# High and low halves of the stationary operands, interleaved word by word in one tile

## The chip, the cores and the metric

The kernel runs on one core of a Trainium2 chip. The metric is the device time of one execution in microseconds (us); smaller is better. Names of engines: PE is TensorE (matmuls), PEld its weight loads, DVE is VectorE, ACT is ScalarE, POOL is GpSimd, SP is SyncE, which issues most DMAs.

## The reference

One pre-norm layer on an input of 256 tokens by 2048 channels, float32. Four token mixers read one combined projection, their outputs are projected, gated, summed, projected again and added to the input.

```python
h = _rms_norm(x, norm_g)
u = jnp.einsum('bsd,dn->bsn', h, w_in)              # 2048 -> 22672 columns
a_in, b_in, b_gate, c_qkv, c_f, c_gate, d_in, d_gate, m_logit = _split(u, IN_SIZES)
y_a = _short_conv_branch(a_in, conv_w)              # 1024 columns each
y_b = _rwkv7_branch(b_in, b_gate, ...)
y_c = _fox_branch(c_qkv, c_f, c_gate, fox_bf)
y_d = _pool_branch(d_in, d_gate, pool_w, pool_scale)
ys = jnp.stack([y_a, y_b, y_c, y_d], axis=2)
proj = jnp.einsum('bskc,kcd->bskd', ys, w_branch)   # four of 1024 -> 2048
gates = jax.nn.sigmoid(m_logit.reshape(bsz, s, N_BRANCH, d) + b_merge)
merged = jnp.sum(gates * proj, axis=2)
x = x + jnp.einsum('bsd,de->bse', merged, w_out)    # 2048 -> 2048
# and a final _rms_norm(x, final_g)
```

## The kernel before

The 256 tokens are two blocks of 128 (`NB = 2`). Activations are the stationary operand of every large matmul: a slice of 128 channels (k) by 128 tokens is loaded as weights. The weight matrices are the moving operand, 512 columns at a time (`CH`). Each such output of 256 tokens by 512 columns is a chunk (L247 `chunk`).

Float32 accuracy is had from a fast format, fp32r, by splitting each operand in a high part (the value rounded to fp32r) and a low part (the rest). A product of two split operands is made of three matmuls, high times high (L240), high times low (L241) and low times high (L242), which add up in one PSUM tile, `psm`. So a chunk of `w_in` has 16 slices k, two blocks and three products, 96 matmuls, each with a weight load of its own.

Where the high and low parts lie: the moving slices arrive by DMA in `raw` (L259, from SP's queue, two slices a DMA, three buffers), ScalarE rounds them to `wh` (L267) and VectorE subtracts to get `wl` (L268), six buffers each. The stationary parts are two tiles for each operand: `xh` and `xl` for the normalised input (written at L218 by ScalarE and L219 by VectorE, from the PSUM tiles of PE's transposes), and for the branch outputs `yah`, `yal` to `ydh`, `ydl` (L776), written by `split_T` (L771 ScalarE, L772 VectorE). The merged rows are split into `mh` and `ml` (L815, L816), which take the places of `yb`, `yc`, `ya` and a tile of their own, and L831 joins their parts. In all of these tiles the words of one slice lie one behind the other, so that a weight load of 128 words reads 512 bytes in one piece.

Order: the head loads and transposes `x` while the first chunk runs; then come the chunks of the branches, with the work of RWKV (L440) and of the attention (L641) between the chunks on all engines; then `split_T` of three branches and the pool branch (about 750 to 820 us); then the merge, 4 column groups (`dc`) of 4 branches, each with a gate chunk (L740) and a branch chunk of 8 slices (L821), and a `split_T` of 4 slices after each group (L828); last the output projection, 4 chunks (L855). The last of these keeps its split slices in tiles that have become free (`keep`, L847: `xh`, `xl`, `ych`, `ycl`, `ydh`, `ydl`), and runs its second block after its first. The residual `x` is loaded again into `yal` and `ybl` by GpSimd's queue (L842). A scheduler orders the instructions of each engine by priority; the preparation of the moving slices has the highest (`WEIGHTS`).

Of the kernel before, what the change touches and what calls it, by code (L numbers as in the profile page):

```python
# [9 lines left out]
F32 = mybir.dt.float32  # L10
F32R = mybir.dt.float32r
I32 = mybir.dt.int32
AF = mybir.ActivationFunctionType
ALU = mybir.AluOpType
# [3 lines left out]
P = 128  # L18
T = 256
NB = 2  # L20
D = 2048
W = 1024
CH = 512
# [71 lines left out]
def kernel(  # L95
# [27 lines left out]
    nc = tc.nc  # L123
    v = nc.vector
    sc = nc.scalar
# [5 lines left out]
    w_out_v = w_out[0].rearrange("(k p) n -> p k n", p=P)  # L131
# [3 lines left out]
    pers = ctx.enter_context(tc.tile_pool(name="pers", bufs=1))  # L135
    wpool = ctx.enter_context(tc.tile_pool(name="wpool", bufs=1))
    bc_pool = ctx.enter_context(tc.tile_pool(name="bc", bufs=2))
    ynat = ctx.enter_context(tc.tile_pool(name="ynat", bufs=1))
# [22 lines left out]
    ngT = pers.tile([P, D // P], F32, name="ngT")  # L161
# [2 lines left out]
    fss = pers.tile([P, NB, 4], F32, name="fss")  # L164
    frs = pers.tile([P, NB], F32, name="frs")
    fa = pers.tile([P, NB, 16], F32, name="fa")
    xh = pers.tile([P, D // P, T], F32R, name="xh")
    xl = pers.tile([P, D // P, T], F32R, name="xl")
    cst = pers.tile([P, N_CONST], F32, name="cst")

    def load_constants(lo, hi):
# [17 lines left out]
    def flat(t):  # L189
        return t.rearrange("p a b -> p (a b)")  # L190


    gp.memset(ones1, 1.0)

    rw_stack = ExitStack()
# [5 lines left out]
    def x_quarter(q):  # L201

        xt = xin.tile([P, NB, CH], F32, name=f"x{q}")
        nc.sync.dma_start(out=xt, in_=x_v[:, :, q * CH:(q + 1) * CH])
        if q == 0:
            tp = psum_ex("c")
            nc.tensor.transpose(tp[:, 0:16], ng16, ident[:16, :16])
            v.tensor_copy(out=ngT, in_=tp[:, 0:16])
        for k2 in range(2):
            tp = psum_ex("c" if k2 else "r")  # L210
            for j in range(2):
                for b in range(NB):
                    c0 = (2 * k2 + j) * P
                    nc.tensor.transpose(tp[:, j * T + b * P:j * T + (b + 1) * P], xt[:, b, c0:c0 + P], ident)
            for j in range(2):
                k = q * 4 + k2 * 2 + j
                s = tp[:, j * T:(j + 1) * T]
                sc.activation(out=xh[:, k, :], in_=s, func=AF.Copy, scale=ngT[:, k:k + 1])  # L218
                v.scalar_tensor_tensor(out=xl[:, k, :], in0=s, scalar=ngT[:, k:k + 1],  # L219
                                       in1=xh[:, k, :].bitcast(F32), op0=ALU.mult, op1=ALU.subtract)  # L220
        return xt

    def x_squares(q, xt):
# [12 lines left out]
    def products(ps, sth, stl, wh, wl, k, nk, n, b):  # L236
        cols = slice(b * P, (b + 1) * P)
        o = ps[b][:, :n]
        h, l = wh[:, :n], wl[:, :n]
        nc.tensor.matmul(o, lhsT=sth[:, k, cols], rhs=h, start=k == 0, stop=False)  # L240
        nc.tensor.matmul(o, lhsT=sth[:, k, cols], rhs=l, start=False, stop=False)  # L241
        nc.tensor.matmul(o, lhsT=stl[:, k, cols], rhs=h, start=False, stop=k == nk - 1)  # L242

    def new_ps():
        return [ps_main.tile([P, CH], F32, name="psm", tag="psm") for b in range(NB)]
# [1 line left out]
    def chunk(ranges, nk, sth, stl, before=lambda g: None, keep=None):  # L247


        ps = new_ps()  # L250
        n = sum(r[2] for r in ranges)
        for g in range(nk // KG):
            wh, wl = [], []
            with level(WEIGHTS):
                before(g)
                raw = wpool.tile([P, KG, CH], F32, name="raw", bufs=3)
                at = 0
                for wv, c0, w in ranges:
                    nc.sync.dma_start(out=raw[:, :, at:at + w], in_=wv[:, g * KG:(g + 1) * KG, c0:c0 + w])  # L259
                    at += w  # L260
                for j in range(KG):
                    if keep:
                        h, l = keep(g * KG + j)
                    else:
                        h = wpool.tile([P, CH], F32R, name="wh", bufs=6)
                        l = wpool.tile([P, CH], F32R, name="wl", bufs=6)
                    sc.activation(out=h[:, :n], in_=raw[:, j, :n], func=AF.Copy)  # L267
                    v.tensor_tensor(out=l[:, :n], in0=raw[:, j, :n], in1=h[:, :n].bitcast(F32), op=ALU.subtract)  # L268
                    wh.append(h)
                    wl.append(l)  # L270
            for b in range(1 if keep else NB):
                for j in range(KG):
                    products(ps, sth, stl, wh[j], wl[j], g * KG + j, nk, n, b)
        if keep:
            for k in range(nk):
                products(ps, sth, stl, *keep(k), k, nk, n, 1)
        return ps
# [47 lines left out]
    x_norm()  # L325
    rw_stack.close()

    yb = ynat.tile([P, NB, W], F32, name="yb")
    yc = ynat.tile([P, NB, W], F32, name="yc")
    ya = ynat.tile([P, NB, W], F32, name="ya")  # L330


    rw = rw_stack.enter_context(tc.tile_pool(name="rw", bufs=1))
# [5 lines left out]
    lo, hi = slice(0, 64), slice(64, 128)  # L339
# [419 lines left out]
    ytp = ctx.enter_context(tc.tile_pool(name="ytp", bufs=1))  # L759
    yT = {}  # L760

    def split_T(dst, k0, src, nk):

        for k2 in range(0, nk, 2):
            tp = psum_ex("r" if (k2 // 2) % 2 else "z")
            for j in range(2):
                for b in range(NB):
                    nc.tensor.transpose(tp[:, j * T + b * P:j * T + (b + 1) * P],
                                        src[:, b, (k2 + j) * P:(k2 + j + 1) * P], ident)
            hi = flat(dst[0][:, k0 + k2:k0 + k2 + 2, :])  # L770
            sc.activation(out=hi, in_=tp, func=AF.Copy)  # L771
            v.tensor_tensor(out=flat(dst[1][:, k0 + k2:k0 + k2 + 2, :]), in0=tp, in1=hi.bitcast(F32),  # L772
                            op=ALU.subtract)

    def new_yT(nm):
        yT[nm] = [ytp.tile([P, W // P, T], F32R, name=f"y{nm}{i}") for i in "hl"]  # L776
        return yT[nm]

    split_T(new_yT("a"), 0, ya, 8)
    split_T(new_yT("b"), 0, yb, 8)  # L780
# [4 lines left out]
    for hf in range(2):  # L785
# [4 lines left out]
        for g2 in range(2):  # L790
# [6 lines left out]
            for j in range(2):  # L797
                cs = slice((g2 * 2 + j) * P, (g2 * 2 + j + 1) * P)
                tp = psum_ex("c")
# [3 lines left out]
            tp = psum_ex("c")  # L803
            for b in range(NB):
                for j in range(2):
                    nc.tensor.matmul(tp[:, b * T:(b + 1) * T], lhsT=pT[:, j, b * P:(b + 1) * P], rhs=pw[:, j, :],
                                     start=(j == 0), stop=(j == 1))
# [4 lines left out]
        split_T(yTd, hf * 4, yd, 4)  # L812


    mh = [ynat.tile([P, 8, T], F32R, name=n) for n in ("yb", "yc")]  # L815
    ml = [ynat.tile([P, 8, T], F32R, name="ya"), ytp.tile([P, 8, T], F32R, name="ml1")]  # L816
    for dc in range(4):
        mg = wk.tile([P, NB, CH], F32, name="va")
        for n, nm in enumerate("abcd"):
            gt = gate_tile(dc, n)  # L820
            ps = chunk([(w_br_v[n], dc * CH, CH)], W // P, *yT[nm])  # L821
            for b in range(NB):
                if n == 0:
                    v.tensor_tensor(out=mg[:, b, :], in0=ps[b], in1=gt[:, b, :], op=ALU.mult)
                else:
                    v.tensor_tensor(out=gt[:, b, :], in0=ps[b], in1=gt[:, b, :], op=ALU.mult)
                    v.tensor_tensor(out=mg[:, b, :], in0=mg[:, b, :], in1=gt[:, b, :], op=ALU.add)
        split_T([mh[dc // 2], ml[dc // 2]], (dc % 2) * 4, mg, 4)  # L828


    class Parts:  # L831
        def __init__(self, parts):
            self.parts = parts

        def __getitem__(self, key):
            _, k, cols = key
            return self.parts[k // 8][:, k % 8, cols]

    yo = [ytp.tile([P, NB, 1024], F32, name=n) for n in ("yah", "ybh")]
    xr = [ytp.tile([P, NB, 1024], F32, name=n) for n in ("yal", "ybl")]  # L840
    for j in range(2):
        gp.dma_start(out=xr[j], in_=x_v[:, :, j * 1024:(j + 1) * 1024])  # L842

    spare = [t.rearrange("p a b -> p (a b)").rearrange("p (k n) -> p k n", n=CH)
             for t in (xh, xl, *(ytp.tile([P, W // P, T], F32R, name=n) for n in ("ych", "ycl", "ydh", "ydl")))]

    def keep(k):  # L847
        if k < 8:
            return spare[0][:, k, :], spare[1][:, k, :]
        i = 2 + 2 * ((k - 8) // 4)  # L850
        return spare[i][:, k % 4, :], spare[i + 1][:, k % 4, :]

    for dc in range(4):
        fg = bcast(final_g[dc * CH:(dc + 1) * CH])
        ps = chunk([(w_out_v, dc * CH, CH)], D // P, Parts(mh), Parts(ml), keep=keep if dc == 3 else None)  # L855
        cs = slice((dc % 2) * CH, (dc % 2 + 1) * CH)
        for b in range(NB):
            y = yo[dc // 2][:, b, cs]
            v.tensor_tensor(out=y, in0=ps[b], in1=xr[dc // 2][:, b, cs], op=ALU.add)
            sq = wk.tile([P, CH], F32, name="sg", bufs=2)  # L860
            sc.activation(out=sq, in_=y, func=AF.Square, accum_out=fss[:, b, dc:dc + 1])
            if dc < 3:
                v.tensor_tensor(out=y, in0=y, in1=fg, op=ALU.mult)
    for b in range(NB):
        f = frs[:, b:b + 1]
# [4 lines left out]
        for dc in range(4):  # L870
            y = yo[dc // 2][:, b, (dc % 2) * CH:(dc % 2 + 1) * CH]
# [37 lines left out]
```

## Time and profile before

| what | us |
|---|---|
| median of 3 runs | 1433.42 (1430.63 to 1435.92) |
| profiled execution, its own time | 1433.31 |
| its span, first to last instruction | 1431.5 |
| PE busy | 1398.8 (98%) |
| PEld busy | 1146.2 (80%) |
| DVE busy | 984.4 (69%) |
| ACT busy | 736.0 (51%) |

The granted TensorE clock is 0.994 of full on the mean. A matmul's recorded time is longer than the distance between two starts, since matmuls are pipelined: what one costs in a dense stretch is the distance of starts, read from the timeline, and not the mean in a table of groups. A weight load's record overlaps the matmul before it. An f32 matmul (not fp32r) stands in the trace as two passes, each with a weight load.

### The profile page before, as it was taken

How to read it: one execution, taken by the hardware profiler on the slowest of the kernel's cores; microseconds unless marked ns; L12 is line 12 of the kernel's file. 1: busy time of each engine (PE TensorE's matmuls, PEld its weight loads, DVE VectorE, ACT ScalarE, POOL GpSimd, SP SyncE). 2: the span in 40 equal slices, each digit the busy share in tenths (PEclk: the TensorE clock that was granted, in tenths of full speed). 3: DMA queues.
4: the chain of work that ended last, by engine and by line, in shares of the span. 5: the costliest groups of instructions: out<-in, count | busy, mean ns of one | idle time of the engine just before them, and what ended most of it. 6: DMA issues, size and time to landing. Idle time of an engine off the chain costs nothing.

```text
span 1431.5 us, 19581 instructions
## 1 busy us (share of the span) xinstructions
PE 1398.8 (98%) x6913; PEld 1146.2 (80%) x6913; DVE 984.4 (69%) x1719; ACT 736.0 (51%) x1278; POOL 68.5 (5%) x135
## 2 busy tenths in 40 slices
PE   7999999999999899999999999999999999999997
PEld 5887778888887688887888888888888888888885
DVE  4558888589766889669957656666665666556654
ACT  6556644654455455554535544545545545444554
POOL 2110000001001000011000000000000000000000
PEclk9999999999999999999999999999999999999999
DMA  8776545456567646545655566666766666776664
GB/s 254 201 223 200 176 127 175 131 146 204 166 177 201 186 148 177 161 133 177 183 178 147 158 200 203 202 192 201 208 202 194 194 208 198 224 234 201 194 206 147
DMA packets 136626, 266.17 MB, mean 186 GB/s; under 512 B 11577, under 2 KB 15848, under 8 KB 136528
## 3 DMA queue, kind: packets, MB, share of 16 engines
q1 hardware_dynamic: 128768, 240.88, 55.5%
q0 software_dynamic: 7760, 24.04, 6.5%
q8 instruction: 54, 0.88, 0.3%
q14 instruction: 44, 0.36, 0.1%
HBM read 257.44 MB, written 2.10 MB: 181 GB/s over the span
## 4 chain that ended last, share of the span: by engine, by line
PE 67%; DVE 15%; DMA 11%; issue 4%; ACT 2%; POOL 1%; SPq 0%; ACTq 0%; DVEq 0%; POOLq 0%
PE psm L242 20%; PE psm L241 20%; PE psm L240 20%; DVE wl L268 6%; DMA raw<-in_w_in_dram 4%; DVE tm L489 2%; DMA cg<-pz 1%; DVE UQ L491 1%; DVE MT L482 1%; DMA raw<-in_w_out_dram 1%; DMA pv<-ur 1%; ACT wh L267 1%; PE ps_r L468 1%; PE ps_r L541 1%; DMA pv<-uv 1%
## 5 line engine op out<-in xcount | busy, mean ns | idle before, releaser
L267 ACT ACTIVATE wh<-raw 128x512 fp32r<-128x512 f32 (+1 forms) x896 | 545.7, 624 | 535.6 <-PE psm L242 361.3
L268 DVE TENSOR_TENSOR wl<-raw,wh 128x512 fp32r<-128x512 f32 (+1 forms) x896 | 596.5, 681 | 310.7 <-ACT wh L267 309.7
L241 PE MATMUL psm<-wl,xh 128*128 128x512 f32 (+1 forms) x1440 | 563.8, 393 | 7.0 <-DVE wl L268 6.6
L242 PE MATMUL psm<-wh,xl 128*128 128x512 f32 (+1 forms) x1440 | 562.1, 392 | 0.0
L240 PE MATMUL psm<-wh,xh 128*128 128x512 f32 (+1 forms) x1440 | 547.7, 393 | 4.0 <-ACT wh L267 3.4
L241 PEld LDWEIGHTS psm<-wl,xh 128*128 128x128 f32 x1440 | 271.3, 189 | 69.0 <-DVE wl L268 15.8
L240 PEld LDWEIGHTS psm<-wh,xh 128*128 128x128 f32 x1440 | 271.0, 189 | 62.6 <-ACT wh L267 7.2
L242 PEld LDWEIGHTS psm<-wh,xl 128*128 128x128 f32 x1440 | 271.6, 189 | 53.3 <-issue 1.2
L489 DVE TENSOR_TENSOR tm<-UQ,MT 128x16 f32<-128x16 f32 (+30 forms) x124 | 52.2, 421 | 2.0
L491 DVE TENSOR_REDUCE UQ<-tm 128x8 f32<-128x16 f32 (+30 forms) x124 | 36.0, 291 | 1.8
L183 POOL DMA_DIRECT2D row<-in_b_merge_dram x16 | 8.6, 539 | 502.6 <-DVE qa L742 431.8
L482 DVE STREAM_TRANSPOSE MT<-G 32x1024 f32<-32x1024 f32 x16 | 32.0, 2000 | 0.3
L742 DVE SCALAR_TENSOR_TENSOR qa<-psm,rstd,row 128x512 f32<-128x512 f32 x32 | 24.1, 752 | 9.7 <-PE psm L242 9.7
L659 ACT ACTIVATE pt<-pt,mx 128x128 f32<-128x128 f32 (+1 forms) x32 | 14.4, 450 | 23.7 <-DVE mx L657 23.6
L241 PE MATMUL psm<-wl,yah 128*128 128x512 f32 x64 | 24.9, 389 | 0.0
L242 PE MATMUL psm<-wh,yal 128*128 128x512 f32 x64 | 24.9, 389 | 0.0
L241 PE MATMUL psm<-wl,ybh 128*128 128x512 f32 x64 | 24.9, 389 | 0.0
L242 PE MATMUL psm<-wh,ybl 128*128 128x512 f32 x64 | 24.9, 389 | 0.0
L241 PE MATMUL psm<-wl,ych 128*128 128x512 f32 x64 | 24.9, 389 | 0.0
L242 PE MATMUL psm<-wh,ycl 128*128 128x512 f32 x64 | 24.9, 389 | 0.0
L241 PE MATMUL psm<-wl,ydh 128*128 128x512 f32 x64 | 24.9, 389 | 0.0
L242 PE MATMUL psm<-wh,ydl 128*128 128x512 f32 x64 | 24.9, 389 | 0.0
(378 smaller groups left out, 1365.7 us busy)
## 6 DMA issues: line engine op xcount, KB each, us to landing
raw<-in_w_in_dram SPq DMA_DIRECT2D x344, 512.0 KB, 4.1
raw<-in_w_branch_dram SPq DMA_DIRECT2D x64, 512.0 KB, 4.9
raw<-in_w_out_dram SPq DMA_DIRECT2D x32, 512.0 KB, 4.6
row<-in_b_merge_dram POOLq DMA_DIRECT2D x16, 256.0 KB, 4.3
raw<-in_w_in_dram SPq DMA_DIRECT2D x8, 328.0 KB, 4.0
raw<-in_w_in_dram SPq DMA_DIRECT2D x8, 312.0 KB, 3.6
x<-in_x_dram SPq DMA_DIRECT2D x4, 512.0 KB, 8.9
cg<-pz POOLq DMA_DIRECT2D x4, 448.0 KB, 4.8
```

Of the source, the lines that this page charges most:

```text
L240: nc.tensor.matmul(o, lhsT=sth[:, k, cols], rhs=h, start=k == 0, stop=False)
L241: nc.tensor.matmul(o, lhsT=sth[:, k, cols], rhs=l, start=False, stop=False)
L242: nc.tensor.matmul(o, lhsT=stl[:, k, cols], rhs=h, start=False, stop=k == nk - 1)
L267: sc.activation(out=h[:, :n], in_=raw[:, j, :n], func=AF.Copy)
L268: v.tensor_tensor(out=l[:, :n], in0=raw[:, j, :n], in1=h[:, :n].bitcast(F32), op=ALU.subtract)
L468: nc.tensor.matmul(gps[par][:, j * P:(j + 1) * P], lhsT=bk(rows, p, e), rhs=ar(rows, p, e), start=True, stop=True)
L482: v.transpose(out=MT[32 * q:32 * q + 32].rearrange("p t (r u) -> p t r u", u=NH), in_=src)
L489: v.tensor_tensor(out=tm[:, :, 0:n], in0=UQ[:, i:32, :].rearrange("p j c -> p c j"), in1=MT[:, i:32, i].unsqueeze(1).to_broadcast([P, 8, n ...
L491: v.tensor_reduce(out=UQ[:, i, :], in_=tm[:, :, 0:n], axis=AX.X, op=ALU.add)
L541: nc.tensor.matmul(ups[lo, hs], lhsT=UF[:, h, e, :], rhs=z[:, hs], start=True, stop=True)
L659: sc.activation(out=pt[:, s], in_=pt[:, s], func=AF.Exp, scale=-1.0, bias=mx[:, b:b + 1], accum_out=sm[:, b:b + 1])
L742: v.scalar_tensor_tensor(out=gt[:, b, :], in0=ps[b], scalar=rstd[:, b:b + 1], in1=bm, op0=ALU.mult, op1=ALU.add)
```

## The change

Every stationary operand becomes one tile whose last axis has length 2: index 0 is the high word, index 1 the low word of the same element. So the high words of a slice lie 8 bytes apart, with the low words between them. `parts` returns lists of views with that stride; `products`, ScalarE and VectorE use these. `xh` and `xl` become `xT`; `yah` and `yal` become `yaT`, and so on. `ya`, `yb` and `yc` become parts of one tile `ybca`, so that the interleaved `m` (12 of its 16 slices) can take its place as a whole; the other four slices are in `m3`. The tiles that the end of the kernel reuses (`yo`, `xr`, `spare`) are cut from the new ones; within these the moving slices `wh` and `wl` lie in one piece as before. The arithmetic and the instructions stay the same.

```diff
-    xh = pers.tile([P, D // P, T], F32R, name="xh")
-    xl = pers.tile([P, D // P, T], F32R, name="xl")
+    xT = pers.tile([P, D // P * T, 2], F32R, name="xT")
...
+    def parts(t, nk):
+
+        return [[t[:, k * T:(k + 1) * T, i] for k in range(nk)] for i in range(2)]
+
+    xh, xl = parts(xT, D // P)
...
-                sc.activation(out=xh[:, k, :], in_=s, func=AF.Copy, scale=ngT[:, k:k + 1])
-                v.scalar_tensor_tensor(out=xl[:, k, :], in0=s, scalar=ngT[:, k:k + 1],
-                                       in1=xh[:, k, :].bitcast(F32), op0=ALU.mult, op1=ALU.subtract)
+                sc.activation(out=xh[k], in_=s, func=AF.Copy, scale=ngT[:, k:k + 1])
+                v.scalar_tensor_tensor(out=xl[k], in0=s, scalar=ngT[:, k:k + 1],
+                                       in1=xh[k].bitcast(F32), op0=ALU.mult, op1=ALU.subtract)
...
-        nc.tensor.matmul(o, lhsT=sth[:, k, cols], rhs=h, start=k == 0, stop=False)
-        nc.tensor.matmul(o, lhsT=sth[:, k, cols], rhs=l, start=False, stop=False)
-        nc.tensor.matmul(o, lhsT=stl[:, k, cols], rhs=h, start=False, stop=k == nk - 1)
+        nc.tensor.matmul(o, lhsT=sth[k][:, cols], rhs=h, start=k == 0, stop=False)
+        nc.tensor.matmul(o, lhsT=sth[k][:, cols], rhs=l, start=False, stop=False)
+        nc.tensor.matmul(o, lhsT=stl[k][:, cols], rhs=h, start=False, stop=k == nk - 1)
...
-    yb = ynat.tile([P, NB, W], F32, name="yb")
-    yc = ynat.tile([P, NB, W], F32, name="yc")
-    ya = ynat.tile([P, NB, W], F32, name="ya")
+    ybca = ynat.tile([P, 3, NB, W], F32, name="ybca")
+    yb, yc, ya = (ybca[:, i] for i in range(3))
...
-            hi = flat(dst[0][:, k0 + k2:k0 + k2 + 2, :])
+            hi, lo = (dst[:, (k0 + k2) * T:(k0 + k2 + 2) * T, i] for i in range(2))
             sc.activation(out=hi, in_=tp, func=AF.Copy)
-            v.tensor_tensor(out=flat(dst[1][:, k0 + k2:k0 + k2 + 2, :]), in0=tp, in1=hi.bitcast(F32),
-                            op=ALU.subtract)
+            v.tensor_tensor(out=lo, in0=tp, in1=hi.bitcast(F32), op=ALU.subtract)
...
-        yT[nm] = [ytp.tile([P, W // P, T], F32R, name=f"y{nm}{i}") for i in "hl"]
-        return yT[nm]
+        t = ytp.tile([P, W // P * T, 2], F32R, name=f"y{nm}T")
+        yT[nm] = parts(t, W // P)
+        return t
...
-    mh = [ynat.tile([P, 8, T], F32R, name=n) for n in ("yb", "yc")]
-    ml = [ynat.tile([P, 8, T], F32R, name="ya"), ytp.tile([P, 8, T], F32R, name="ml1")]
+    m = [ynat.tile([P, 12 * T, 2], F32R, name="ybca"), ytp.tile([P, 4 * T, 2], F32R, name="m3")]
+    mh, ml = (p + q for p, q in zip(parts(m[0], 12), parts(m[1], 4)))
...
-    yo = [ytp.tile([P, NB, 1024], F32, name=n) for n in ("yah", "ybh")]
-    xr = [ytp.tile([P, NB, 1024], F32, name=n) for n in ("yal", "ybl")]
+    ends = [ytp.tile([P, 2, NB, 1024], F32, name=n) for n in ("yaT", "ybT")]
+    yo, xr = ([t[:, i] for t in ends] for i in range(2))
```

## Rows read from the trace of the kernel before

**Rows 1.** The page's first part: busy us, share of the span, instructions.
```profile
PE 1398.8 (98%) x6913; PEld 1146.2 (80%) x6913; DVE 984.4 (69%) x1719; ACT 736.0 (51%) x1278; POOL 68.5 (5%) x135
```
**Rows 2.** Windows: stretch, length, busy us by engine (instructions), clock; then of psm alone.
```profile
0.00:60.00 60.00, 50.01 (x220) 39.40 (x221) 32.73 (x59) 34.48 (x73) 10.80 (x24) 1.00 0.77 231
60.00:750.00 690.00, 676.09 (x3671) 550.22 (x3670) 533.82 (x1022) 358.22 (x658) 46.01 (x90) 0.99 0.59 172
750.00:1387.00 637.00, 637.00 (x2872) 528.07 (x2871) 397.39 (x603) 324.27 (x513) 11.67 (x21) 1.00 0.66 198
1387.00:1431.50 44.50, 35.71 (x156) 28.53 (x154) 20.45 (x38) 19.02 (x36) 0.00 (x0) 0.93 0.47 159
...
60.00:750.00 690.00, 575.35 (x2403) 438.32 (x2402) 15.61 (x21) 29.20 (x47) 0.99 0.59 172
750.00:1387.00 637.00, 625.47 (x2732) 510.96 (x2731) 51.02 (x71) 3.40 (x5) 1.00 0.66 198
```
**Rows 3.** The chain that ended last, from 740 us: shares by line.
```profile
by line: PE psm L242 30.9%; PE psm L240 30.8%; PE psm L241 30.8%; DMA raw<-in_w_out_dram 2.3%; PE ps_r L768 0.8%; PE ps_z L768 0.8%; PE ps_c L806 0.5%; DVE xl L268 0.4%; DVE wl L268 0.3%; PE ps_c L800 0.3%; ACT xh L267 0.2%; PE ps_z L558 0.
```
**Rows 4.** Waits (us, times, longest): first 750 to 1390 us, then 60 to 750.
```profile
ACT wh L267 <- PE psm L242: 266.5, 208, 3.0
...
ACT wh L267 <- PE psm L242: 94.8, 72, 4.4
...
PE psm L241 <- DVE wl L268: 5.4, 11, 0.8
```
**Rows 5.** Timeline of PE, 512 columns: start us, us, engine, line, out<-in.
```profile
999.80 0.39 PE L241 MATMUL psm<-wl,ybh 128*128 128x512 f32 x1
...
1005.02 0.39 PE L242 MATMUL psm<-wh,ybl 128*128 128x512 f32 x1
...
1012.95 0.39 PE L241 MATMUL psm<-wl,xh 128*128 128x512 f32 x1
```
**Rows 6.** Timeline of PE, 328 columns.
```profile
65.67 0.31 PE L242 MATMUL psm<-wh,xl 128*128 128x328 f32 x1
...
70.13 0.31 PE L242 MATMUL psm<-wh,xl 128*128 128x328 f32 x1
```
**Rows 7.** f32 passes: timeline of PE, and their lines (ns min/median/max).
```profile
797.56 1.89 PE L806 MATMUL ps_c<-qk,sg 128*128 128x256 f32 x8
...
L806 PE MATMUL ps_c<-qk,sg x32: 377/379/483, 722.0 to 799.1; 128*128 128x256 f32 x32
...
465.82 1.88 PE L420 MATMUL ps_r<-s,cst 128*128 128x512 f32 x4
...
L420 PE MATMUL ps_r<-s,cst x8: 590/591/592, 139.6 to 467.1; 128*128 128x512 f32 x8
```
**Rows 8.** Groups of weight loads: busy us, mean ns of one; then one in the timeline.
```profile
L242 PEld LDWEIGHTS psm<-wh,xl 128*128 128x128 f32 x1440 | 271.6, 189 | 53.3 <-issue 1.2
L541 PEld LDWEIGHTS ps_r<-z,UF 64*64 64x64 f32 x128 | 8.0, 135 | 2.5 <-issue 1.8 <-ACT wh L267 0.7
L806 PEld LDWEIGHTS ps_c<-qk,sg 128*128 128x128 f32 x32 | 5.8, 189 | 0.9
...
1005.02 0.19 PEld L241 LDWEIGHTS psm<-wl,ybh 128*128 128x128 f32 x1
```
**Rows 9.** VectorE: lines L219 and L772 (ns min/median/max), groups of L489 and L810.
```profile
L219 DVE SCALAR_TENSOR_TENSOR xl<-ps_r,ngT,xh x8: 472/476/484, 9.9 to 26.6; 128x256 fp32r<-128x256 f32 x8
...
L772 DVE TENSOR_TENSOR ycl<-ps_z,ych x2: 683/687/691, 795.4 to 801.7; 128x512 fp32r<-128x512 f32 x2
...
L489 DVE TENSOR_TENSOR tm<-UQ,MT 128x256 f32<-128x256 f32 x4 | 2.7, 664 | 0.0
...
L810 DVE TENSOR_TENSOR pz<-ps_c,row 128x256 f32<-128x256 f32 x8 | 2.9, 417 | 3.1 <-PE ps_c L806 1.9 <-PE ps_z L768 1.1
```
**Rows 10.** Lines L768 and L771: first and last start of the last reads and first writes.
```profile
L768 PE MATMUL ps_z<-cst,yc x8: 271/272/273, 793.9 to 800.8; 128*128 128x128 f32 x8
...
L771 ACT ACTIVATE yb<-ps_z x2: 580/580/581, 947.9 to 1079.4; 128x512 fp32r<-128x512 f32 x2
```

More of the change, by code (lines that the diff above doesn't have):

```diff
@@ L827 @@
                     v.tensor_tensor(out=mg[:, b, :], in0=mg[:, b, :], in1=gt[:, b, :], op=ALU.add)
[L828 to L837, printed above, removed]
-    yo = [ytp.tile([P, NB, 1024], F32, name=n) for n in ("yah", "ybh")]
-    xr = [ytp.tile([P, NB, 1024], F32, name=n) for n in ("yal", "ybl")]
+        split_T(m[dc // 3], dc % 3 * 4, mg, 4)
+    ends = [ytp.tile([P, 2, NB, 1024], F32, name=n) for n in ("yaT", "ybT")]
+    yo, xr = ([t[:, i] for t in ends] for i in range(2))
     for j in range(2):
         gp.dma_start(out=xr[j], in_=x_v[:, :, j * 1024:(j + 1) * 1024])
-    spare = [t.rearrange("p a b -> p (a b)").rearrange("p (k n) -> p k n", n=CH)
-             for t in (xh, xl, *(ytp.tile([P, W // P, T], F32R, name=n) for n in ("ych", "ycl", "ydh", "ydl")))]
+    spare = [t.rearrange("p t i -> p (t i)").rearrange("p (k i n) -> p k i n", i=2, n=CH)
+             for t in (xT, *(ytp.tile([P, W // P * T, 2], F32R, name=n) for n in ("ycT", "ydT")))]
     def keep(k):
[L848 to L851, printed above, removed]
+        t = spare[0][:, k] if k < 8 else spare[k // 4 - 1][:, k % 4]
+        return t[:, 0], t[:, 1]
     for dc in range(4):
         fg = bcast(final_g[dc * CH:(dc + 1) * CH])
-        ps = chunk([(w_out_v, dc * CH, CH)], D // P, Parts(mh), Parts(ml), keep=keep if dc == 3 else None)
+        ps = chunk([(w_out_v, dc * CH, CH)], D // P, mh, ml, keep=keep if dc == 3 else None)
         cs = slice((dc % 2) * CH, (dc % 2 + 1) * CH)
```

## The prediction

> **What bounds the kernel now.** I read the top of the page first: TensorE is busy 1398.8 of 1431.5 us, VectorE 984.4, ScalarE 736.0 [rows 1]. The windows by stretch say where this is tight [rows 2]. From 750 to 1387 us TensorE is busy in all 637.0 us; from 60 to 750 us it lacks 13.9 us of 690; in the first 60 us it lacks 10.0, and after 1387 us 8.8. The chain cut to the part behind 740 us shows what the end waits for [rows 3]: it is the three products of a chunk (L240 to L242), 31% of that part each; VectorE has under 1%, and DMAs of `w_out` 2.3%. So in the middle of the kernel a nanosecond per matmul is a nanosecond of the end. The other producers aren't late there: ScalarE waited 266.5 us for TensorE to free a slice buffer between 750 and 1390 us, and 94.8 us between 60 and 750 us, while matmuls of L241 waited 5.4 us for VectorE [rows 4].
>
> The one number that matters is then the spacing of the fast matmuls (fp32r, 128x512), 5472 of them: three lines of 1440 on `xh` and `xl` for `w_in` [rows 8], and by the loops 768 for `w_branch` and 384 for `w_out`. The timeline gives it [rows 5]: 59 starts from 999.80 to 1012.95 us are 58 spacings of 226.7 ns. The granted clock is 1.00 there [rows 2], the 2.4 GHz level, so 512 columns are 213.3 ns and 13.4 ns are left over. For the 328-column chunk [rows 6] 31 starts from 65.67 to 70.13 us give 148.7 ns; 328 columns are 136.7, and 12.0 are left over. So the remainder hardly depends on the columns: it comes once per matmul, and each matmul has one weight load.
>
> **Is it the price of changing weights?** The plain f32 matmuls do the same change of 128 weights and don't pay it [rows 7]. Eight passes of L806 (256 columns) span 1.89 us with one of 0.38, which is 7 spacings of 215.7 ns. Four passes of L420 (512 columns) give (1.88 - 0.59)/3 = 430. The 256 columns between them cost 214, 0.84 ns each, two cycles of 2.4 GHz (0.833); so 213.3 and 426.7 are the columns, and 2.4 and 3.3 are left. Their weight loads last 189 ns, as the fast ones' do [rows 8]. What differs is the pace of the moving operand: one word per 0.417 ns against 0.833. The weight load's own pace is (189 - 135)/64 = 0.84 ns a column, from 128 and 64 columns [rows 8]. So where both streams walk through memory at the same pace about 3 ns are left over, and where the moving one walks twice as fast as the weights 13.4 are. The spacing is that regular over all 58 [rows 5], so it is no chance clash with ScalarE, VectorE or DMA.
>
> **The change, part by part.** No instruction is added or removed and none is moved to another queue; addresses change.
>
> *The weight loads.* All 5472 read every second word. The number of columns stays 128. As the weight load then covers 8 bytes in 0.84 ns and the moving operand 4 bytes in 0.417, both walk at one pace, as in the f32 passes. I take this as the nearest row and price the remainder at 2.4 to 3.3 ns, a spacing of 216.2, which is 10.5 ns less. Bounds: nothing gained, 0; and lost, the remainder doubled, since twice as much memory is touched per load, 240.1 ns, +13.4. No row has a weight load with gaps, so the sign is not shown; the pace argument is the only difference between the rows that pay and those that don't, and so I lean to it. How slow could a load get unseen? In the steady stretch it starts with the previous matmul (load and matmul both at 1005.02 us) [rows 5, 8]. A load half as fast would take up 128 x 1.67 = 214 ns of each spacing, an estimate from that pace, still under 226.7.
>
> A rule speaks against this sum. The Trainium skill ("SBUF — State Buffer", Specifications, and its note on cachelines under the DMA port swizzle) says that two hits on a 16-byte line are enough for full bandwidth, so that fp32 may be strided by up to four for free; a stride of two would then change nothing, and the sum would be 0. The Trainium skill ("TensorE: Matmul & The Clock Gate", What happens when you issue a matmul) adds that the weights have a read port of their own and don't take bandwidth from the running matmul; its warm spacing, N/2.4 + 2.5 ns, would be 215.8, while the row has 226.7, so here something not in that rule is paid.
>
> Where does the gain reach the end? The windows count the matmuls on `psm` [rows 2]: 2732 from 750 to 1387 us, 2403 from 60 to 750. In the first all of it counts: 2732 x 10.5 = 28.7 us. In the second the chain passes through VectorE and DMA in places and TensorE has 13.9 us of gaps; of 2403 x 10.5 = 25.2 us I count three quarters, 18.9, by the waits of rows 4 (ends: half, 12.6, and all, 25.2). The first 60 us and the end after 1387 us wait for DMAs [rows 3]; what TensorE saves there waits longer: 0 (at most (5472 - 2732 - 2403) x 10.5 = 3.5). Slices must then come 4.9% faster; VectorE is busy 397.4 of 637 us and DMA 0.66 between 750 and 1387 us [rows 2], so the next thing late isn't reached there. Sum: -47.6 us.
>
> *The writers.* 32 instructions at L218/L219 and 48 at L771/L772 write every second word, and VectorE's read `hi` so. Packed, the VectorE ones take 476 and about 687 ns [rows 9]. The nearest strided row is L489, 256 elements read with gaps on both sides in 664 ns, against L810, 256 elements, 417 [rows 9]: 1.6 times. 24 x 0.6 x 0.687 = 10 us and 16 x 0.6 x 0.476 = 4.6 us of VectorE at the most, 0 at the least; ScalarE's at the same factor 24 x 0.6 x 0.580 [rows 10] = 8.4 us, of 312.7 that it is free there [rows 2]. The first lies in the stretch where VectorE is free 239.6 us [rows 2] and TensorE turns from the four transposes to another chunk; I count 0, and 10 if that cover were gone. The 4.6 lie in the head beside the loads of `x`, counted 0.
>
> *Waits.* If the two halves of a tile were taken for one range, a matmul with `hi` would wait for the `lo` write too, one VectorE instruction later (0.48 us). In the head, 16 slices of `x`: 0 to 7.6 us; elsewhere the operands are written long before use. I take 0. The joined tile `ybca` comes free with the last transpose of `yc` (800.8 us) and is first rewritten at 947.9 us [rows 10]: 147 us of room. `yaT` and `ybT` come free after the same last L242 as `yal` and `ybl` do now: 0.
>
> Against the profiled execution's 1433.3 us (a span of 1431.5, in the table above, and 1.8 around it; the median of the runs is 1433.4, 0.1 away): 1433.3 - 47.6 = 1385.7 us. With half and all of the middle stretch and the head it is 1392 and 1376; if only half of the remainder goes, 1409.
>
> **The rivals.**
> *It stays* (mechanism: the 13.4 ns belong to the fast form itself, for example to the handover of weights at that pace, and gaps cost nothing). For it: the remainder is steady over 58 spacings and nearly the same at 328 and 512 columns, as a fixed step would be. Against: the f32 passes with the same loads. Time: 1433, or up to 1443 if a part of the writers or the waits comes through.
> *It gets slower* (mechanism: each piece of memory that a load touches delays the moving stream, and there are twice as many). Place: every fast matmul behind the first 60 us. Price: 13.4 x (2732 + 2403) = 68.8 us, 1502 us. It decides as soon as the load counts pieces and not words. For it: the remainder comes once per load whatever the columns are, and the moving stream has no slack at one word per cycle. Against: the f32 passes fetch as many weights and pay 2.4, though their moving stream has slack.
> *It doesn't do what it says*: if the load were issued as before from a copy there would be one more instruction; the diff has none. Not weighed.
>
> **How the numbers follow.** Less remainder, in whole or in part (1373 to 1412): 0.50. It stays: 0.28, of which 0.25 within 0.5% (7 us, about what a measurement of this kernel can tell from no change) and 0.03 above it. Doubled remainder, or a load slower than twice: 0.19. Slower through writers and waits alone: 0.03. So faster 0.50, same 0.25, slower 0.25. The likeliest case's own range is 1373 to 1412; the range for 8 in 10 goes on to 1445 and leaves out the doubled remainder.
>
> **What would show it.** Right: spacings near 216 ns in a timeline like rows 5, TensorE still without gaps from 60 us to the last chunk, and the third chunk of the `w_out` loop ending some 45 us earlier. A spacing of 226.7 means that the remainder is the form's own, 240 that touched memory counts. Loads far above 189 ns, or gaps ahead of L240 put down to VectorE, would mean that I mispriced the reads or the waits.

## The result

The changed kernel takes 1454.99 us (median of four runs, 1454.06 to 1457.24), the kernel before 1432.03 beside it (1429.58 to 1435.92). The ratio is 1.016, with a 95% interval of 1.0133 to 1.0188: slower by some 23 us, where 1385.7 us was forecast, with a range of 1373 to 1445.

The profile after has the page's first part and the windows that answer to [rows 1, 2]:

```profile
span 1453.5 us, 19582 instructions
PE 1424.4 (98%) x6913; PEld 1178.1 (81%) x6913; DVE 987.9 (68%) x1719; ACT 738.4 (51%) x1278; POOL 68.5 (5%) x135
...
60.00:750.00 690.00, 679.91 (x3648) 562.36 (x3647) 532.92 (x1018) 358.01 (x656) 45.99 (x90) 1.00 0.58 172
750.00:1387.00 637.00, 637.00 (x2810) 528.87 (x2809) 389.11 (x587) 316.73 (x497) 11.13 (x20) 1.00 0.64 193
```

The span grew by 22.0 us and TensorE's busy time by 25.6. Between 750 and 1387 us TensorE is still busy without a gap, but it starts 2810 instructions there and not 2872. The instructions are the same, and on each engine they come in the same order in both traces, TensorE's 6913 matmuls too. So in this stretch it is no added wait; each matmul takes longer. The timeline shows how much longer, first in the dense part (53 starts, 52 spacings, of matmuls on `ybT` and `xT`), then in the chunk of 328 columns (25 starts, 24 spacings); these answer to [rows 5, 6]:

```profile
1013.81 0.39 PE L245 MATMUL psm<-wl,ybT 128*128 128x512 f32 x1
...
1025.94 0.39 PE L246 MATMUL psm<-wh,xT 128*128 128x512 f32 x1
...
66.76 0.31 PE L244 MATMUL psm<-wh,xT 128*128 128x328 f32 x1
...
70.36 0.31 PE L244 MATMUL psm<-wh,xT 128*128 128x328 f32 x1
```

The first give 12.13 us / 52 = 233.3 ns, where the kernel before has 226.7; the second 3.60 / 24 = 150.0 ns, nearly as before (148.7). At 2.4 GHz 233.3 ns are 560 cycles and 226.7 are 544, so at 512 columns the remainder, what a spacing has beyond one cycle for each column, rose from 32 to 48 cycles.

Where in the kernel do the 22 us arise? Two marks are enough: the first write of `split_T` for the first branch, and the first use of an output chunk. Here are both in the kernel before, then in the changed one (lines as the page numbers them; min/median/max ns, then first and last start):

```profile
L771 ACT ACTIVATE yah<-ps_z x2: 587/594/600, 769.9 to 776.4; 128x512 fp32r<-128x512 f32 x2
...
L859 DVE TENSOR_TENSOR yah<-psm,yal x4: 691/691/692, 1355.5 to 1378.7; 128x512 f32<-128x512 f32 x4
```

```profile
L774 ACT ACTIVATE yaT<-ps_z x2: 623/630/638, 774.0 to 780.9; 128x512 fp32r<-128x512 f32 x2
...
L852 DVE TENSOR_TENSOR yaT<-psm,yaT x4: 692/692/692, 1376.0 to 1399.8; 128x512 f32<-128x512 f32 x4
```

The first mark comes 4.1 us later, the second 20.5. The dense part between the marks holds about as many fast matmuls as all before it, and it brings 16.4 us against 4.1. The 4.1 is a rough number: in two kernels of the next section whose input is packed the first mark lies at 769.3 and 772.5 us, and in one whose input is interleaved at 775.0.

### The profile page after: what moved, and what is told of

Same layout as the page of the kernel before. It is cut to its first block, busy times and chain, and to the rows that moved or that the text cites. A ratio compares the mean times of both kernels' runs of the same rounds, so it can differ in the third digit from the quotient of the medians.

```text
span 1453.5 us, 19582 instructions
## 1 busy us (share of the span) xinstructions
PE 1424.4 (98%) x6913; PEld 1178.1 (81%) x6913; DVE 987.9 (68%) x1719; ACT 738.4 (51%) x1278; POOL 68.5 (5%) x135
## 4 chain that ended last, share of the span: by engine, by line
PE 76%; DVE 10%; DMA 7%; issue 3%; ACT 2%; POOL 1%; SPq 0%; ACTq 0%; DVEq 0%; POOLq 0%
PE psm L245 23%; PE psm L246 23%; PE psm L244 23%; DVE wl L272 4%; DMA raw<-in_w_in_dram 2%; DVE MT L485 2%; DMA cg<-pz 1%; DVE tm L492 1%; DMA raw<-in_w_out_dram 1%; ACT wh L271 1%; DVE UQ L494 1%; PE ps_r L471 1%; PE ps_z L561 1%; PE ps_r L544 1%; DMA pv<-ur 1%
## 5 line engine op out<-in xcount | busy, mean ns | idle before, releaser
L245 PE MATMUL psm<-wl,xT 128*128 128x512 f32 (+1 forms) x1440 | 568.6, 396 | 3.7 <-DVE wl L272 3.3
L246 PE MATMUL psm<-wh,xT 128*128 128x512 f32 (+1 forms) x1440 | 568.0, 396 | 0.0
L244 PE MATMUL psm<-wh,xT 128*128 128x512 f32 (+1 forms) x1440 | 553.4, 397 | 4.1 <-ACT wh L271 3.8
L245 PEld LDWEIGHTS psm<-wl,xT 128*128 128x128 f32 x1440 | 279.8, 194 | 61.3 <-DVE wl L272 8.6
L244 PEld LDWEIGHTS psm<-wh,xT 128*128 128x128 f32 x1440 | 279.4, 195 | 61.3 <-ACT wh L271 7.2
L246 PEld LDWEIGHTS psm<-wh,xT 128*128 128x128 f32 x1440 | 280.1, 195 | 52.6 <-issue 1.2
L245 PE MATMUL psm<-wl,ybca 128*128 128x512 f32 x72 | 28.3, 395 | 0.0
L246 PE MATMUL psm<-wh,ybca 128*128 128x512 f32 x72 | 28.2, 394 | 0.0
L244 PE MATMUL psm<-wh,ybca 128*128 128x512 f32 x72 | 27.5, 395 | 0.0
L246 PE MATMUL psm<-wh,ydT 128*128 128x512 f32 x64 | 25.2, 394 | 0.0
L245 PE MATMUL psm<-wl,ybT 128*128 128x512 f32 x64 | 25.2, 394 | 0.0
L246 PE MATMUL psm<-wh,ycT 128*128 128x512 f32 x64 | 25.2, 394 | 0.0
L245 PE MATMUL psm<-wl,ydT 128*128 128x512 f32 x64 | 25.2, 394 | 0.0
L245 PE MATMUL psm<-wl,yaT 128*128 128x512 f32 x64 | 25.2, 394 | 0.0
```

The costliest lines, as they stand in the source:

```text
L244: nc.tensor.matmul(o, lhsT=sth[k][:, cols], rhs=h, start=k == 0, stop=False)
L245: nc.tensor.matmul(o, lhsT=sth[k][:, cols], rhs=l, start=False, stop=False)
L246: nc.tensor.matmul(o, lhsT=stl[k][:, cols], rhs=h, start=False, stop=k == nk - 1)
```

## Experiments

**Is it the gaps, or the joined tiles?** Two kernels undo a part. In the first all tiles stay joined but each slice has 256 high words in one piece and then 256 low words:

```diff
     def parts(t, nk):

-        return [[t[:, k * T:(k + 1) * T, i] for k in range(nk)] for i in range(2)]
+        f = t.rearrange("p t i -> p (t i)").rearrange("p (k i n) -> p k i n", i=2, n=T)
+        return [[f[:, k, i] for k in range(nk)] for i in range(2)]
```

(and `split_T` writes these pieces). What was expected:

> The changed kernel with all its joined tiles, but within each tile 256 high words of a slice lie in one piece and then its 256 low words; the weight loads are packed again. Theory (the gaps in the weight load cost): back to the kernel before, 1432 us within 4, spacing 226.7 ns. Rival (joined tiles, their waits or their places in memory cost): stays near 1455 us with a spacing near 233 ns or with new gaps.

Measured: 1434.9 us, ratio 1.0005 (0.999 to 1.0019). From 999.66 to 1011.90 us it has 54 spacings of 226.7 ns. So the joined tiles, the later release of `ybca` and the residual's place cost nothing that can be told from 0, and the loss lies in the step of the words.

The second keeps only the input interleaved, and a third only the branch outputs and merged rows; each uses the packed `parts` above for the other operands.

> As the changed kernel, but only the normalised input is interleaved (4320 of 5472 fast matmuls); the branch outputs and the merged rows lie in blocks. Theory (the gaps cost 6.7 ns a matmul and count in full from matmul 2700 on, to a quarter before): behind it lie some 1550 matmuls on x and 1152 on the others, so 1432 + 4.5 + 1550 x 6.67 ns = 1447 us, and both spacings, 233.3 on x and 226.7 on the others, stand in one trace. Rival (the cost is one of the whole program, for example of where the tiles lie): one spacing for all.

> As the changed kernel, but the normalised input lies in blocks; the branch outputs and merged rows are interleaved (1152 of 5472 fast matmuls, all in the dense part). Theory (6.7 ns a matmul there, in full): 1433.5 + 1152 x 6.67 ns = 1441 us, and the first 2700 fast matmuls take as long as in the kernel before. Rival (the cost sits in the stretch before, or is one of the program): 1433 or 1455.

Measured: 1448.41 us, ratio 1.0100 (1.0083 to 1.0116), and 1439.11 us, ratio 1.0051 (1.0034 to 1.0069). That is 14.3 and 7.3 us, 21.6 together, of the 22.9 that the ratio of the changed kernel makes. In the timeline of the kernel with only the input interleaved both kinds stand behind one another: 45 spacings between the first two lines, 43 between the last two:

```profile
1004.80 0.39 PE L251 MATMUL psm<-wh,ybT 128*128 128x512 f32 x1
...
1015.00 0.39 PE L251 MATMUL psm<-wh,ybT 128*128 128x512 f32 x1
...
1024.79 0.39 PE L250 MATMUL psm<-wl,xT 128*128 128x512 f32 x1
...
1034.83 0.39 PE L249 MATMUL psm<-wh,xT 128*128 128x512 f32 x1
```

10.20 / 45 = 226.7 ns for packed weights and 10.04 / 43 = 233.5 for interleaved ones. So the cost goes with each matmul whose weights have gaps. In the other kernel the first mark stays (769.3 us, 0.6 earlier than before the change), as expected, and the stretch between the marks is 5.7 us longer; with only the input interleaved it is 10.8 us longer, and 5.7 and 10.8 make the 16.4 of the whole change to 0.1 us.

**The cost by itself.** A probe kernel runs sections of 64 matmuls with nothing beside them.

```diff
+    for i in range(64):
+        nc.tensor.matmul(two_a, lhsT=S[:, c0:c0 + 256:2], rhs=M[:, i % 4, 0:512], start=i == 0, stop=i == 63)
```

> No part of the reference is computed here but a stream of matmuls: sections of 64 fast (fp32r) matmuls back to back, each with a weight load of 128 words taken at a step of 1, 2, 4, 8 or 16 words and a moving operand of 256 to 512 packed words; then a step of 2 beginning at an odd word, packed weights beginning 8 bytes into a 16-byte piece, the same weights each time, a moving operand at a step of 2, and the f32 form with a step of 1 and 2. ScalarE, VectorE and the DMA queues are nearly idle. Theory (the gaps in the weight load cost): packed 512 columns 226.7 ns from start to start, a step of 2 gives 233.3 as in the changed kernel, a step of 4 more than that, and 8 and 16 as much as 4 or more. Rival (not the gaps but the other edits, the joined tiles and their addresses): 226.7 at every step. Rival (pieces of memory counted by the load, as the prediction had it): 32 cycles over the columns at a step of 1, 64 at 2, 128 at 4, so 226.7, 240, 267 ns. If the cost is one per load, it is the same 6.7 ns at 448, 384 and 328 columns; the trace of the changed kernel has 150 ns at 328 columns, as before, so a dependence on the columns is expected there.

A row is one section: start, length, and x64; the spacing is the length without the last matmul (0.31 to 0.41 us), over 63; the granted clock is 1.00. The names say the step of the weights (one, two, four, eight words) and then the columns: a is 512, b 448, d 328; `plain` is the f32 form, 512 columns in two passes.

```profile
29.18 14.67 PE L164 MATMUL one_a<-M,S 128*128 128x512 f32 x64
43.69 15.09 PE L168 MATMUL two_a<-M,S 128*128 128x512 f32 x64
...
73.56 15.21 PE L176 MATMUL four_a<-M,S 128*128 128x512 f32 x64
88.60 15.80 PE L180 MATMUL eight_a<-M,S 128*128 128x512 f32 x64
...
119.30 13.38 PE L188 MATMUL one_b<-M,S 128*128 128x448 f32 x64
132.51 13.18 PE L192 MATMUL two_b<-M,S 128*128 128x448 f32 x64
...
167.74 9.76 PE L204 MATMUL one_d<-M,S 128*128 128x328 f32 x64
177.34 9.76 PE L208 MATMUL two_d<-M,S 128*128 128x328 f32 x64
...
260.57 55.12 PE L232 MATMUL plain_one<-M,S 128*128 128x512 f32 x128
315.52 55.10 PE L236 MATMUL plain_two<-M,S 128*128 128x512 f32 x128
```

One word and two words at 512 columns are 226.7 and 233.3 ns, as in the two kernels, with ScalarE, VectorE and DMA at rest. But four words cost only 235.0, eight 244.5, sixteen 235.3; at 328, 384 and 256 columns a step of two costs nothing (150.0 ns both); and at 448 columns the interleaved weights are the *cheaper* ones, 203.3 against 206.7 ns. The f32 form doesn't care (429.2 both). The weight loads themselves (mean ns of one) lengthen in another way:

```profile
L180 PEld LDWEIGHTS eight_a<-M,S 128*128 128x128 f32 x64 | 15.7, 329 | 0.0
L176 PEld LDWEIGHTS four_a<-M,S 128*128 128x128 f32 x64 | 15.1, 310 | 0.0
L168 PEld LDWEIGHTS two_a<-M,S 128*128 128x128 f32 x64 | 12.4, 193 | 2.6
L164 PEld LDWEIGHTS one_a<-M,S 128*128 128x128 f32 x64 | 12.0, 188 | 2.5
```

193 against 188 ns at a step of two: the load with gaps is nearly as fast, and there is room for it. What gets longer is the spacing of the matmuls that run beside it. By the cacheline rule of the Trainium skill ("SBUF — State Buffer", Door 1: The DMA port swizzle) a step of two words keeps two hits a line and is free; for the load's own length the trace nearly agrees, for the spacing of the matmuls it doesn't, and there the measurement decides.

**A beat, or pieces touched?** The first theory, that gaps cost, can't make gaps cheaper at 448 columns. The second probe asked whether it is the place where the two streams of reads, of the weights and of the moving operand, meet. If they get in each other's way at some distances and not at others, as a beat between two rhythms, then the start addresses must count too.

> Again no part of the reference but sections of 64 fast matmuls with the other engines nearly idle. The first probe gave 544 cycles at 2.4 GHz for packed weights and 512 columns (32 over the columns), 560 with a step of 2, 553.6 with packed weights 8 bytes off a 16-byte piece, and at 448 columns 496 packed against 488 with a step of 2. Theory (the extra cost is a beat between the two streams of reads: it depends on where they meet, so on start addresses, columns and step, and not simply on how much memory a load touches): packed weights moved by 16, 32 or 64 bytes cost 544 again, by 4 or 8 bytes some 550 to 560; a moving operand off by 4 or 8 bytes costs more as well, even with packed weights; at 464, 480 and 504 columns a step of 2 is sometimes dearer and sometimes cheaper than packed. Rival (touched pieces): 64 weights cost half of the remainder, 528 cycles packed and 536 to 544 with a step of 2, 32 weights 520; start addresses change it by one piece at the most, 1 cycle; a step of 2 is never cheaper. Rival (a fixed handover of the fast form): 544 at every number of weights, and no start address changes it.

`off_two` and `off_sixteen` have packed weights that start 2 and 16 words later, in `mov_one` the moving operand starts one word later, in `both_two` both start 2 words later; `cols_half_one` loads only 64 weights:

```profile
29.24 14.68 PE L165 MATMUL one_a<-M,S 128*128 128x512 f32 x64
...
58.63 14.92 PE L173 MATMUL off_two<-M,S 128*128 128x512 f32 x64
...
103.25 15.10 PE L185 MATMUL off_sixteen<-M,S 128*128 128x512 f32 x64
118.18 15.30 PE L189 MATMUL mov_one<-M,S 128*128 128x512 f32 x64
...
178.01 14.96 PE L205 MATMUL both_two<-M,S 128*128 128x512 f32 x64
192.81 14.90 PE L209 MATMUL cols_half_one<-M,S 128*64 128x512 f32 x64
```

Packed weights 16 words off cost 233.4 ns, as much as interleaved ones, with no gap at all; 2 words off 230.7. Half the weights cost 230.0 and not less. So the rival of touched pieces falls (it wanted 220 ns for 64 weights), and so does a fixed handover (it wanted no effect of the start). My own theory was wrong in two points: weights moved by 16, 32 or 64 bytes were expected to cost 544 cycles again, and cost 560; and a step of two was expected to be cheaper at some of 464, 480 and 504 columns, where it was dearer at the first two (by some 2 and 3 ns) and the same at the third.

The same in the real kernel: everything in blocks, but the input starts two words behind the start of its tile.

```diff
-    xT = pers.tile([P, D // P * T, 2], F32R, name="xT")
+    xT0 = pers.tile([P, D // P * T * 2 + 8], F32R, name="xT")
+    xT = xT0[:, 2:2 + D // P * T * 2].rearrange("p (t i) -> p t i", i=2)
```

> All halves in blocks, nothing interleaved, but the tile of the normalised input begins 8 bytes off a 16-byte piece. Theory (where the reads meet decides): the probe's 230.7 ns for matmuls on x, so +4.0 ns for 1548 of them in the dense part, 6.2 us, and about a third of 2700 x 4.0 = 10.8 us before, 1443 us in all, without any gap in a load. Rival (gaps are what costs): 1434 us, as with halves in blocks.

Measured: 1442.68 us, ratio 1.0074 (1.0059 to 1.0089), as expected, and 44 spacings on `xT` give 231.1 ns, while 40 on `ybT` in the same trace give 226.8:

```profile
1000.31 0.39 PE L247 MATMUL psm<-wl,ybT 128*128 128x512 f32 x1
...
1009.38 0.39 PE L247 MATMUL psm<-wl,ybT 128*128 128x512 f32 x1
...
1019.77 0.39 PE L247 MATMUL psm<-wl,xT 128*128 128x512 f32 x1
...
1029.94 0.39 PE L247 MATMUL psm<-wl,xT 128*128 128x512 f32 x1
```

So a start alone costs in the kernel too, without any gap. That the size came out is in part luck. The edit makes the tile eight words longer, and every tile behind it, the moving slices among them, lies 32 bytes further on; so the weights on `xT` begin 24 bytes before the place of the moving slices, and not 8 bytes behind it as in `off_two`. No probe has that pair.

**Where is the best place?** The third probe moved the starts of packed weights (`st`), of the moving operand (`mv`) and of both (`bo`).

> Sections of 64 fast matmuls, packed weights, the other engines nearly idle, as in the two probes before. Swept are the start of the weights within 512 bytes (64 to 496 bytes off), the start of the moving operand (64 bytes to 1 KB off), both by the same amount, both by different amounts, and 472 to 496 columns. So far every start at a multiple of 512 bytes gave 544 cycles for 512 columns, every other one 552 to 568. Theory (a beat of the two read streams with 544 as its best case): no pair of starts is under 544, and a moving operand off by 512 bytes or 1 KB gives 544. Rival (the multiples of 512 bytes are only one point of the beat): some pair of starts gives less than 544, down to 518, what the plain f32 passes pay; then a kernel with such starts would gain up to 2.9 ns to 10.8 ns a matmul.

```profile
29.31 14.67 PE L165 MATMUL one_a<-M,S 128*128 128x512 f32 x64
43.81 15.09 PE L169 MATMUL st_sixteen<-M,S 128*128 128x512 f32 x64
...
88.27 14.67 PE L181 MATMUL st_sixtyfour<-M,S 128*128 128x512 f32 x64
...
147.24 14.67 PE L197 MATMUL st_hundredtwentyfour<-M,S 128*128 128x512 f32 x64
...
206.22 14.69 PE L213 MATMUL mv_sixtyfour<-M,S 128*128 128x512 f32 x64
...
264.70 14.89 PE L229 MATMUL bo_four<-M,S 128*128 128x512 f32 x64
...
293.98 14.69 PE L237 MATMUL bo_sixteen<-M,S 128*128 128x512 f32 x64
```

Either stream moved by 64 words (256 bytes) is as good as none, 226.7 and 227.0 ns; the weights alone by 16 words are 233.4; both by the same 16 words are 227.0 again. So at 512 columns, with shifts that are multiples of 64 bytes, it is the difference of the two starts within 256 bytes that counts, to about 1 ns. With finer shifts the difference alone doesn't say it. Both streams moved by the same 2 words cost 231.3 ns (`both_two`) and by the same 4 words 230.0 (`bo_four`), though the difference is 0, while the same 8, 16 or 32 words cost 227.0 to 227.5; and weights that lie 4 words before the moving operand within 256 bytes cost 226.7 when the weights were moved (by 124 words, `st_hundredtwentyfour`) and 231.7 when the moving operand was (`mov_four` of the second probe). The expectation of the last probe below says that the cost depended only on the difference; that is too strong.

No pair was under 544 cycles. In the kernel before, as it is built, all slices of the weights and of the moving operand start 96 bytes behind a multiple of 512 bytes, the same place for both, and it has the 544 cycles. The rival, a kernel with better starts, has nothing to offer among the starts that were tried.

The last probe did the same for interleaved weights.

> Sections of 64 fast matmuls of 512 columns, nothing else; all but one have weights with a step of 2, as in the changed kernel. Swept is the start of the weights (8 to 512 bytes off) or of the moving operand (16 to 512 bytes off). With packed weights the cost depended only on the difference of the two starts within 256 bytes: 544 cycles at 0, 549 to 568 elsewhere. Theory (a beat, and the interleaved load has one too): the cost changes with the difference of starts, is the same again at 256 and 512 bytes, and if some difference gives 544, the loss of the changed kernel could have been avoided by placing its tiles. Rival (an interleaved load of 128 weights covers 1 KB, four times 256 bytes, and so meets the moving reads at every difference): 556 to 564 at every start, and no placement undoes it.

```profile
44.97 15.09 PE L169 MATMUL two_a<-M,S 128*128 128x512 f32 x64
...
119.32 14.89 PE L189 MATMUL st_sixteen<-M,S 128*128 128x512 f32 x64
...
208.38 15.10 PE L213 MATMUL st_sixtyfour<-M,S 128*128 128x512 f32 x64
```

With a step of two all 24 pairs lie between 551.8 and 560.5 cycles; 16 words off is the best, 229.9 ns, and 64 words off repeats 233.3. Neither theory was quite right: the start counts here too, and 256 bytes bring back the same spacing, but the effect is shallow and never reaches 544. Better places would have saved about half of the loss and no more; that kernel was not run, but by these spacings its best case is slower than the kernel before.

**What is a matmul worth before 780 us?** In the kernel before, 200 of 2400 fast matmuls ahead of the branch transposes were left out.

```diff
-        nc.tensor.matmul(o, lhsT=stl[:, k, cols], rhs=h, start=False, stop=k == nk - 1)
+        if not (short[0] and k % 4 == 2):
+            nc.tensor.matmul(o, lhsT=stl[:, k, cols], rhs=h, start=False, stop=k == nk - 1)
```

> The kernel before, packed. In the 25 chunks ahead of the branch transposes the product low times high is left out for 4 of 16 slices, 200 of 2400 fast matmuls; the result is that much less exact. It measures what a matmul is worth in that part. 184 of them have 512 columns and 16 have 328 or less: 184 x 226.7 + 16 x 150 ns = 44 us of TensorE. Theory (only about a third of the chain runs through fast matmuls there): 13 to 17 us less, some 1418 us. Rival (TensorE paces that part as its busy share says): 33 to 44 us less, 1390 to 1400 us. Nothing changes behind 780 us.

Measured: 1429.32 us, ratio 0.9976 (0.9959 to 0.9994): 3.4 us for 44 us of TensorE, less than either theory said. Its window from 60 to 750 us:

```profile
60.00:750.00 690.00, 664.07 (x3555) 536.38 (x3554) 546.99 (x1044) 369.03 (x680) 45.88 (x90) 0.99 0.62 181
```

TensorE has 12 us more of gaps here than in [rows 2]. Two things blur the price. The scheduler set instructions in another order for this kernel: its first mark comes at 786.1 us, 16.2 later than in the kernel before, and its second at 1348.6, 6.9 earlier. And the mean granted clock was 0.981 to 0.990 of full in its ten runs, where it was 0.995 to 0.998 in the thirteen of the kernel before beside them. So part of what was saved may have gone to a slower clock, and the 3.4 us are a low value for the price. How much is due to each is open.

## Why the prediction was wrong

**The weight loads: the sign.** The step that failed is the pace argument. It was right that the remainder is no plain price of changing weights and that it belongs to the fast form. It then took the f32 passes [rows 7] for the nearest row and inferred that two streams at one pace leave 3 ns over; +10.5 ns were booked as gain where 6.7 were lost. The f32 passes don't tell this: they are blind to the step (429.2 ns both ways), and they differ from the fast form in more than the pace. What the runs showed in its place is that the remainder depends on the two starts, on the step and on the columns, from 32 cycles up to 56 among packed starts at 512 columns. That the two streams of reads get in each other's way fits all of this, but it is argued; no run shows what happens in memory. All 58 spacings of [rows 5] had the same low remainder because every start in that kernel sits at the best place that the probes found. That a number is the lowest of its kind can't be seen in a trace that holds only that number. The reading that the remainder hardly depends on the columns came from 512 and 328 alone: packed weights at the same start have 48 cycles at 448 columns and 40 at 480.

**The rival on the other side** had the right sign and a place that held, but the mechanism and the size were wrong: it priced the doubled remainder, +13.4 ns and 1502 us. Half of the weights cost more and not less, and a step of four less than twice that of two. 6.7 ns x 2732 matmuls from 750 to 1387 us are 18.3 us; the marks show 16.4 us up to the first output chunk, and 1.5 us more arise behind it.

**"It stays"** had 0.28, and its example, a fixed handover, is refuted by the starts. At 328, 384 and 256 columns its forecast held: a step of two costs nothing there.

**Where the gain reaches the end: three quarters.** In the stretch up to 780 us I let 18.9 of 25.2 us through, on the busy share and the waits of rows 4. A loss of 6.7 ns for each of its 2400 matmuls would be 16 us, and some 4 arrived, about a quarter; in the other direction 3.4 of 44. The chain cut to 60 to 780 us warns of it. In the kernel before, then in the changed one, then in the one with only the input interleaved, which has the same weights as the changed one in this stretch:

```profile
by line: PE psm L241 11.5%; PE psm L242 11.5%; PE psm L240 11.3%; DVE wl L268 10.3%; issue 7.9%; DMA raw<-in_w_in_dram 6.9%; DVE tm L489 4.1%; DMA cg<-pz 2.8%; DVE UQ L491 2.5%; DVE MT L482 2.3%; PE ps_r L468 1.7%; ACT wh L267 1.4%; PE ps_r
```

```profile
by line: PE psm L245 16.9%; PE psm L244 16.8%; PE psm L246 16.8%; DVE wl L272 6.4%; issue 6.2%; DMA raw<-in_w_in_dram 3.1%; DVE MT L485 3.1%; DMA cg<-pz 2.8%; DVE tm L492 2.6%; DVE UQ L494 1.5%; PE ps_r L471 1.5%; PE ps_z L561 1.2%; PE ps_r
```

```profile
by line: PE psm L249 12.4%; PE psm L250 12.3%; PE psm L251 12.3%; DVE wl L277 8.1%; issue 6.4%; DVE tm L497 3.5%; DMA raw<-in_w_in_dram 3.2%; DMA cg<-pz 2.8%; DVE MT L490 2.6%; DVE UQ L499 2.1%; PE ps_r L476 1.5%; PE ps_z L566 1.2%; PE ps_r
```

Fast matmuls are 34% of the chain before, 51% after and 37% in the third. With a packed input they are 38% with the halves in blocks and 27% with only the branch outputs and merged rows interleaved. So the share differs by over 10 points from trace to trace with the same weights, and the rise from 34 to 51 can't be called the effect of the change. What holds is that in the packed kernels 62 to 73% of the chain runs through something else, in the kernel before VectorE's `wl` (10.3%) and the DMAs of `w_in` (6.9%) first, and that a quarter of the loss arrived; that those other parts took up the rest fits, but is not shown. TensorE was "busy" for 98% of that stretch all the same. A record of 0.39 us reaches beyond the next start, 0.227 us later, so a busy share can't show short gaps.

**Writers.** The bound of 1.6 times was far too high. VectorE's interleaved writes take what they took (`ycT` at L775, median 688 ns, against 687 in [rows 9]), ScalarE's some 7% more (`ybca` at L774, 621 ns, against 580 in [rows 10]):

```profile
L774 ACT ACTIVATE ybca<-ps_z x3: 617/621/621, 956.7 to 1227.3; 128x512 fp32r<-128x512 f32 x3
...
L775 DVE TENSOR_TENSOR ycT<-ps_z,ycT x2: 684/688/692, 800.0 to 806.5; 128x512 fp32r<-128x512 f32 x2
```

Counting 0 was right. **Waits** were right too: with the halves in blocks the joined tiles cost nothing, and no order changed.

## What to carry to other kernels

A row in which all instances look alike says nothing about a layout that none of them has; where the sign hangs on that, a probe of sixty matmuls settles it, and until then the two signs should stand as equals. Keep the weights of back-to-back fp32r matmuls of 512 columns packed, and let weights and moving operand start at the same place within 256 bytes, at one that is a multiple of 32 bytes: every such pair tried here had 226.7 to 227.5 ns, and interleaved weights 229.9 to 233.5. And don't price a change of one engine by its busy share. Its share of the chain in that stretch is nearer, but still only a rough upper value: 34% in the kernel before, where 26% of a loss and 8% of a saving arrived.

## What was not expected of the hardware

Two reads that are told as independent disturb each other. By the Trainium skill ("TensorE: Matmul & The Clock Gate", What happens when you issue a matmul) weight loads have a port of their own and take nothing from the running matmul; the traces agree for the f32 form, where a step of two changed nothing, and for fp32r they don't: the start of the weights alone moved the spacing from 226.7 to 233.4 ns, and the start of the moving operand by one word to 236.7. Its 2.5 ns over the columns were never reached with fp32r in these runs; the least in the probes was 32 cycles, 13.3 ns, at 256, 328, 384, 496 and 512 columns, and in the kernel before 12.0 ns at 328 [rows 6]. A moving operand at a step of two words cost double, 453 ns:

```profile
231.58 29.17 PE L228 MATMUL mov_two<-M,S 128*128 128x512 f32 x64
```

Why the best case is 32 cycles, and what in memory has the period of 256 bytes, stays open.
